# Column sums of squares held for all four of their squares, and the sixth pair of up blocks in seven products

## The chip, the cores and the metric

The kernel runs on one core of one Trainium2 chip. The metric is the device time of one execution in microseconds (us). A difference of about 0.3% is the least that a measurement of this kernel can tell from none. The engines are named as the profile names them: PE (TensorE; PEld are its weight loads), ACT (ScalarE), DVE (VectorE), POOL (GpSimd) and SP (SyncE, here a DMA queue). Matmuls have a fixed operand (128x128, loaded first) and a moving one.

## The reference, cut to what matters

One inference step of a two-layer decoder on 512 prompt tokens and 8 x 4 sample tokens (TOK = 544 columns, D_MODEL = 1024, D_FF = 2816). Every layer is a token mixer (causal pooling in layer 0, an HGRN2 recurrence in layer 1) and a gated feed-forward part with a short convolution, with RMS norms around both. All is float32.

```python
def rmsnorm(x, g):
    r = lax.rsqrt(jnp.mean(xf * xf, axis=-1, keepdims=True) + EPS)
    return (xf * r * g.astype(jnp.float32)).astype(x.dtype)

def conv_ffn(h, ctx, w_up, conv_w, conv_b, w_down):
    u = h @ w_up                                   # 1024 -> 2 * 2816
    full = jnp.concatenate([ctx.astype(u.dtype), u], axis=1)
    c = conv_b + sum(full[:, j:j + L] * conv_w[j] for j in range(CONV_W))
    gate, val = jnp.split(c, 2, axis=-1)
    y = (jax.nn.gelu(gate, approximate=True) * val) @ w_down

def trunk(...):
    for li in range(DEPTH):
        h = rmsnorm(x, norm_mix_pre[li])
        m = pool_mixer(...) or hgrn_mixer(...)
        x = x + rmsnorm(m, norm_mix_post[li])
        h = rmsnorm(x, norm_ffn_pre[li])
        m, st = conv_ffn(h, ffn_ctx[li], ...)
        x = x + rmsnorm(m, norm_ffn_post[li])
```

## The kernel before, in words

**Layout and precision.** Activations lie transposed: channels on 128 partitions, the 544 tokens along the free axis, eight such tiles for D_MODEL. A float32 matmul is done as three in the faster fp32r form: a value is split into a high part (ACT rounds it) and a low part (DVE subtracts the high part), and high x high, high x low and low x high are summed in PSUM (`mm3`, lines 516 to 520). Weights are split in the same way, in units of up to 128x512 (`ensure_units`, lines 444 to 477): SP loads a raw tile, ACT writes `wh`, DVE writes `wl`. There are ten buffers of each, and the code keeps nine units ahead of PE. Some blocks are split by transfers instead (`by_dma`, lines 430 to 432, with the windows `DW` of line 56): POOL issues a DMA that writes `wh`, ACT writes the negative of `wh` into `wl`, and POOL issues a second DMA that adds the weight to it (lines 460 to 463). DVE has no part in that.

**The feed-forward part** (`ffn`, from line 917). Its 22 pairs of up blocks (gate and value) come in parts of 6, 4, 4, 3 and 5 (`PARTS`), each followed in time by the down blocks of the part before. Pairs 0 to 2 are done by `group` in two column halves, pairs 3 to 5 of the first part by `block` (lines 522 to 530): 8 k-tiles x 2 halves x 3 products for each block, so 96 matmuls of 256 or 288 columns for a pair. All later pairs (`j >= SEVEN`, which is 6) are done by `seven` (lines 1058 to 1094): a 2 x 2 scheme of Winograd's kind with seven products of 4 k-tiles x 3, so 84 matmuls of 272 columns for a pair. That needs sums and differences of the operands, made once by `operands` (lines 1029 to 1046: `a`, `w`, and the `z` and `s` parts, which are kept whole in `hold`), and split by `both` (lines 1048 to 1050: ACT the high part, DVE the low part). It needs sums of the weights too, made by `seventh` (lines 479 to 498) with accumulating transfers into a raw tile `B_` and one DVE addition each for units 2 and 5; unit 6 uses a raw tile `C_`. Units 0, 4 and 6 of the seven are plain quarters of the weights. The operands are made while pairs 4 and 5 run (lines 1136 to 1139). The high and low parts of `z` and `s` (lines 1140 to 1144) go into tiles that the ordinary pairs still read, so they start when the last ordinary matmul is done; in the first product that uses `z` (the fifth) PE needs them.

**The residual steps** (`Residual`, lines 732 to 798) join two parts of a layer: for each half of the columns the mixer's or feed-forward's output is normalized, added to x (DVE), scaled and split (ACT `xh` or `oh`, DVE `xl` or `k`), and squared (ACT). `colsums` (lines 650 to 655) adds the squares over channels on PE: for each of the eight tiles one matmul with 32 columns of ones, tile k into the 32 partitions at `k % 4 * 32`, so that four neighbouring tiles use four different column quarters of PE and the second four are added to the first. Their total goes through ACT (`t<-pr`), a reciprocal root on DVE and PE again, and becomes `R`, by which the up blocks' results are multiplied. In the profile these matmuls are `pr<-t,cs 128*32`; the trace shows two records for each.

**The order of work** is planned. `Plan.record` (lines 127 to 159) notes every instruction with what it must follow; `Plan.emit` (lines 192 to 312) plays them through with a cost for each and picks, for the engine that is free first, the ready instruction with the longest tail of work behind it; PE takes matmuls that touch `pr` first (`urgent`, line 255). The order within each engine's queue is fixed by that; on the chip each instruction then waits for its own data alone. `plan.after(x)` (lines 118 to 123) adds, for the planner, that the next instruction follows the last writer of x. In `colsums` each of the four matmuls is held for its own square and for the last square of its four (line 654).

Of the kernel before, what the change touches and what calls it, by code (L numbers as in the profile page):

```python
# [11 lines left out]
F32 = _mybir.dt.float32  # L12
F32R = _mybir.dt.float32r
I32 = _mybir.dt.int32
AF = _mybir.ActivationFunctionType
ALU = _mybir.AluOpType

P = 128
# [18 lines left out]
PARTS = (6, 4, 4, 3, 5)  # L37

MIX = ((4, 4, 0, 0), (3, 3, 2, 0), (3, 3, 2), (2, 2, 2, 2, 0))

SEVEN = PARTS[0]

EARLY = 5

# [9 lines left out]

COLD = 7.0
DW = ((2, 12), (3, 32), (3, 12))
PACE = 0.25
HK = (0, 0, 0, 3, 5, 7, 27, 39)
GRP_U = 6
# [286 lines left out]
def trunk_step(ctx: ExitStack, tc: _tile.TileContext, xT, xp, xs, spool, s0, fctx, par, gb0, cst, bands,  # L346
               pw, wup, wdn, win, wout, yT, yB, o_pp, o_ps, o_hp, o_hs, o_ff):
    nc = tc.nc
    plan = Plan(tc)
    PE, DVE, ACT, POOL, SP = (plan.engine(*e) for e in (  # L350
        ("PE", nc.tensor), ("DVE", nc.vector), ("ACT", nc.scalar), ("POOL", nc.gpsimd), ("SP", nc.sync)))
# [10 lines left out]
    def tt(shape=(P, TOK), dt=F32):  # L362
        return tp.tile(list(shape), dt, tag="t", name="t")
# [11 lines left out]
    stream = []  # L375
# [3 lines left out]
    def add_up(li, j):  # L379
        up_i[li, j] = len(stream)  # L380
        if j < SEVEN:
            stream.append((wup[li, j], KT))
# [45 lines left out]
    bases = (0, min(hin_i.values()), up_i[1, 0])  # L428

    def by_dma(i):  # L430

        return any(lo <= i - b < hi for (lo, hi), b in zip(DW, bases))
    prepared = {}
    special = {}
    units = [(i, q) for i, (_, kc) in enumerate(stream) for q in range(-(-kc // 4))]
# [2 lines left out]
    raws, casts = {}, {}  # L438
    sums = {}

    def ensure(upto):
        ensure_units(unit0.get(upto + 1, len(units)) - 1)

    def ensure_units(upto):
        while nxt[0] <= min(upto, len(units) - 1):
            i, q = units[nxt[0]]
            nxt[0] += 1
            src, kc = stream[i]
            chunks = prepared.setdefault(i, [])
            n = min(4, kc - 4 * q) * P  # L450
            if i in special:
                sp, at = special[i]
                wh, wl = sp[at + q], sp[at + 2 + q]
            else:
                wh = wp.tile([P, 4 * P], F32R, tag="wh", name="wh", bufs=10)
                wl = wp.tile([P, 4 * P], F32R, tag="wl", name="wl", bufs=10)
            chunks.append((wh, wl))
            if by_dma(i):

                h, l, w = wh[:, 0:n], wl[:, 0:n], src[:, q * 4 * P:q * 4 * P + n]  # L460
                POOL.dma_start(h, w)
                ACT.activation(l, h.bitcast(F32), AF.Identity, scale=-1.0)
                POOL.dma_start(l, w, accum_op=ALU.add)
                continue
            if kc == 28:
                r = seventh(i, q)
            else:
                if q == 0:
                    raws[i] = tt((P, 512)) if kc * P <= 512 else wp.tile([P, KT * P], F32, tag="raw", name="raw")
                    if kc * P <= 512 and nxt[0] - 1 - EARLY in casts:  # L470

                        plan.held = {casts[nxt[0] - 1 - EARLY]}
                    SP.dma_start(raws[i][:, 0:kc * P], src)
                r = raws[i][:, q * 4 * P:q * 4 * P + n]
            casts[nxt[0] - 1] = len(plan.ops)
            ACT.activation(wh[:, 0:n], r, AF.Identity)
            DVE.tensor_tensor(wl[:, 0:n], r, wh[:, 0:n].bitcast(F32), op=ALU.subtract)

    def seventh(i, q):

        H = 4 * P
        lo, hi = slice(0, H), slice(H, 2 * H)
        w0, w1 = stream[i][0]
        if q == 0:
            B_, A_ = [wp.tile([P, KT * P], F32, tag="raw", name="raw") for _ in range(2)]
            raws[i] = A_, B_, sums[i % 2] if sums else tt((P, H))
            SP.dma_start(B_[:, hi], w1[:, lo])
            POOL.dma_start(B_[:, hi], w1[:, hi], accum_op=ALU.add)  # L490
            SP.dma_start(A_, w0)
            SP.dma_start(B_[:, lo], w0[:, lo])
            POOL.dma_start(B_[:, lo], w1[:, lo], accum_op=ALU.add)
            SP.dma_start(raws[i][2], w1[:, hi])
        A_, B_, C_ = raws[i]
        if q in (2, 5):
            DVE.tensor_tensor(B_[:, hi], B_[:, hi], A_[:, lo if q == 2 else hi], op=ALU.add)
        return (A_[:, lo], B_[:, hi], B_[:, hi], B_[:, lo], A_[:, hi], B_[:, hi], C_)[q]
# [23 lines left out]
    def block(i, rH, rL, kc, cut=HT, tick=None):  # L522

        t = ps2()
        for k in range(kc):
            for hf, sl in enumerate((slice(0, cut), slice(cut, TOK))):
                mm3(t[:, hf, 0:sl.stop - sl.start], i, k, rH, rL, sl, k == 0, k == kc - 1)
                if tick:
                    tick()
        return t  # L530
# [80 lines left out]
    def x_of(k, sl=slice(0, TOK)):  # L611
        return xt[k // 2][:, k % 2, sl]
# [3 lines left out]
    def pcol(off):  # L616
        return prm[:, off:off + 1]
# [32 lines left out]
    def colsums(pn, sqs, ks):  # L650

        for k in ks:
            j = k % 4 * 32
            plan.after(sqs[ks[-1]])
            PE.matmul(pn[j:j + 32], ones[:, 0:32], sqs[k], start=(k < 4), stop=(k >= 4), skip_group_check=True)

    def spread(dg, out):
# [259 lines left out]
    def ffn(li, XH, XL, res, enter, mtag, leave, n_ahead, homes, hv=HV):  # L917
# [35 lines left out]
        def evac_full(u, us, ps):  # L953
            DVE.tensor_tensor(u[:, 2:2 + SEQ].rearrange("p (a c) -> p a c", a=2), ps[:, :, 0:HP],
                              R[:, 0:SEQ].rearrange("p (a c) -> p a c", a=2), op=ALU.mult)
            DVE.tensor_tensor(us[:, :, 2:6], ps[:, 1, HP:HP + NS].rearrange("p (b t) -> p b t", t=NL), Rs, op=ALU.mult)
# [72 lines left out]
        def operands(k, out):  # L1029

            za, hold = tt(), out["hold"]
            zb, w, s_ = hold[:, k], hold[:, 6 + k % 2], hold[:, 4 + k // 2, U[k % 2]]
            for z, f in ((za, k), (zb, k + 4)):
                DVE.scalar_tensor_tensor(z, x_of(f), pcol(gn + f), R, op0=ALU.mult, op1=ALU.mult)
                SP.dma_start(yT[:, f], x_of(f))
            DVE.tensor_tensor(w[:, U[0]], za[:, U[1]], zb[:, U[1]], op=ALU.subtract)
            DVE.tensor_tensor(w[:, U[1]], za[:, U[0]], za[:, U[1]], op=ALU.subtract)
            DVE.tensor_tensor(za[:, U[1]], za[:, U[0]], w[:, U[0]], op=ALU.subtract)
            DVE.tensor_tensor(s_, zb[:, U[0]], za[:, U[1]], op=ALU.subtract)
            both(out["a", k], za)  # L1040
            if k % 2:

                h, l = (big.tile([P, 2, TOK], F32R, tag=f"X{q}", name="op") for q in (k // 2, 2 + k // 2))
                for e in range(2):
                    out["w", k - 1 + e] = h[:, e], l[:, e]
                    both(out["w", k - 1 + e], hold[:, 6 + e])

        def both(hl, src):
            ACT.activation(hl[0], src, AF.Identity)
            DVE.tensor_tensor(hl[1], src, hl[0].bitcast(F32), op=ALU.subtract)  # L1050

        def operand(q, k):
# [46 lines left out]
        def ahead_units(u):  # L1099
            ensure_units(min(u + 9, end))  # L1100
# [14 lines left out]
        def up(j):  # L1115
            if j >= SEVEN:
                seven(j)
                return
            for b in (j, NPAIR + j):
                i = up_i[li, b]  # L1120
                ahead_units(unit0[i])
                t = block(i, rH, rL, KT, HP)
                u, us = new_u(b, None if li == 0 and j < 8 else t[:, 0, 0:HP])
                evac_full(u, us, t)
                finish(u, us, b)
# [4 lines left out]
            y = [ys[starts[pi] + k] for k in range(PARTS[pi])]  # L1130
            do_down(pi, o, block(i, lambda k, sl: y[k][0][:, sl], lambda k, sl: y[k][1][:, sl], PARTS[pi]), None)

        up(GRP_U // 2)
        out, late = homes()
        out["hold"] = big.tile([P, KT, TOK], F32, tag=mtag, name="hold")
        for j in range(GRP_U // 2 + 1, PARTS[0]):
            for k in range(2):
                operands(2 * (j - GRP_U // 2 - 1) + k, out)
            up(j)
        late(out)  # L1140
        for k in range(4):
# [3 lines left out]
        rest = rp.tile([P, TOK], F32, tag="R", name="sums")  # L1145
        sums.update({0: rest[:, 0:4 * P], 1: fst[:, 2 * NPAIR * 18:2 * NPAIR * 18 + 4 * P]})
        mtile = big.tile([P, KT, TOK], F32, tag=mtag, name="m")
        for pi in range(1, len(PARTS)):
            for kind, q in mixed(pi):
                if kind == "down":  # L1150
                    down(pi - 1, q)
                else:
                    up(q)
            if pi == 1 and li == 0:
                plan.after(mtile[:, KT - 1, :])
                lower_bounds()
                POOL.memset(A, 0.0)
                POOL.memset(qm, 0.0)
                POOL.memset(Asp, 0.0)
# [6 lines left out]
        n, j0 = PARTS[LP], starts[LP]  # L1166
# [13 lines left out]
        for o in range(2, KT - GRP_D):  # L1180
            i = dn_i[li, LP, o]
# [449 lines left out]
    for kind, h in hgrn_order[GRP_U:]:  # L1631
        i = hin_i[kind, h]
        ensure(i + LOOK)
        while kind == "g" and "on" not in hd[h]:
            pending.pop(0)()
        pace[1] = PACE
        t = block(i, rH, rL, KT, HP, tick)
# [154 lines left out]
```

## Time and profile before

| | us |
|---|---|
| median of 3 runs | 1161.19 (1158.90 to 1162.99) |
| the profiled execution, its own time | 1161.18 |
| its span, first to last instruction | 1159.3 |
| PE busy | 1143.8 |
| DVE busy | 870.1 |
| ACT busy | 685.8 |
| POOL busy | 406.4 |

The profiled execution's time is the median of the runs to 0.01 us; 1.9 us of it lie outside the span. In the profile nearly every instruction has line 312, where the planner issues it, so groups are told by tile names: `out<-in`. `pa` and `ps` are the PSUM tiles of ordinary work, `pr` those of the norms; `op`, `hold`, `k`, `xl` hold operands; `wh` and `wl` the weight parts. A timeline row gives start, length, engine, what was done and, in brackets, idle time before it and what ended that. In the chain of waits each row gives start, length, engine and tile, and xN for N instructions merged.

### The profile page before, as it was taken

The numbers are of one execution on the slowest core, as the hardware profiler recorded it, in microseconds if no ns is written. First come the engines' busy times: TensorE is split into PE (matmuls) and PEld (weight loads), VectorE is DVE, ScalarE is ACT, GpSimd is POOL, SyncE is SP. The second block draws the span as 40 slices with busy tenths as digits, with TensorE's granted clock in tenths as the row PEclk, the third lists the DMA queues.
The fourth block names the chain that finished last, engine by engine and source line by source line (L and its number), as shares of the span: only waits on it lengthen the run. The fifth ranks groups of instructions, "written<-read, shape, count | busy, mean of one in ns | idle before, by whom it ended". The sixth has DMA issues, their size and how long they took to land.

```text
span 1159.3 us, 26118 instructions
## 1 busy us (share of the span) xinstructions
PE 1143.8 (99%) x9860; PEld 1104.2 (95%) x9860; DVE 870.1 (75%) x2068; ACT 685.8 (59%) x1459; POOL 406.4 (35%) x729
## 2 busy tenths in 40 slices
PE   8999999999999999999999999999999999999996
PEld 7789999999999998999999999979999999999996
DVE  6679977988788776576766785458986897878865
ACT  4546555656566575566666764455565665656653
POOL 3435222433443332443443420224621434343322
PEclk9999999999999999999999999999999999999999
DMA  9876167676876765777667642573536767777543
GB/s 317 206 189 133 55 175 178 169 179 171 195 172 159 206 208 115 156 149 162 154 157 154 135 127 101 149 188 79 132 83 187 190 167 180 174 169 192 115 127 77
DMA packets 90397, 183.48 MB, mean 158 GB/s; under 512 B 10522, under 2 KB 17050, under 8 KB 90264
## 3 DMA queue, kind: packets, MB, share of 16 engines
q0 software_dynamic: 48272, 91.90, 40.0%
q1 hardware_dynamic: 41856, 89.88, 23.7%
q8 instruction: 77, 1.26, 0.4%
q14 instruction: 48, 0.39, 0.1%
q10 hardware_dynamic: 144, 0.05, 0.0%
HBM read 156.00 MB, written 12.77 MB: 146 GB/s over the span
## 4 chain that ended last, share of the span: by engine, by line
PE 96%; DMA 1%; DVE 1%; ACT 1%; issue 0%; SPq 0%; POOL 0%; DVEq 0%; ACTq 0%; POOLq 0%
PE pa L312 47%; PE ps L312 46%; PE pr L312 3%; DMA t<-bands 1%; DMA wh<-win 0%; DVE t L312 0%; ACT A L312 0%; DVE x L312 0%; ACT t L312 0%; DVE m L312 0%; SPq L312 0%; DVE c L312 0%; ACT wl L312 0%; POOL t L312 0%; DVEq L1772 0%
## 5 line engine op out<-in xcount | busy, mean ns | idle before, releaser
L312 ACT ACTIVATE wh<-raw 128x512 fp32r<-128x512 f32 (+2 forms) x280 | 163.9, 598 | 158.5 <-PE pa L312 59.7
L312 PE MATMUL pa<-op,wh 128*128 128x272 f32 x1152 | 255.7, 288 | 0.0
L312 PE MATMUL ps<-t,wh 128*128 128x272 f32 x1248 | 236.5, 288 | 0.0
L312 DVE TENSOR_TENSOR wl<-raw,wh 128x512 fp32r<-128x512 f32 (+2 forms) x280 | 179.1, 652 | 75.3 <-ACT wh L312 73.2
L312 PE MATMUL pa<-op,wl 128*128 128x272 f32 x768 | 221.2, 288 | 0.0
L312 PEld LDWEIGHTS ps<-t,wh 128*128 128x128 f32 x1248 | 195.9, 188 | 0.0
L312 PEld LDWEIGHTS pa<-op,wh 128*128 128x128 f32 x1152 | 192.9, 188 | 0.0
L312 PE MATMUL ps<-t,wl 128*128 128x272 f32 x624 | 179.5, 288 | 0.0
L312 POOL COPY fst<-t 128x16 f32<-128x16 f32 (+1 forms) x176 | 92.8, 581 | 246.3 <-DVE t L312 246.2
L312 DVE TENSOR_TENSOR t<-t 128x512 f32<-128x512 f32 (+10 forms) x331 | 138.5, 441 | 45.6 <-ACT t L312 23.7
L312 PE MATMUL ps<-xh,wh 128*128 128x256 f32 (+1 forms) x560 | 165.7, 297 | 0.0
L312 PE MATMUL ps<-xl,wh 128*128 128x256 f32 (+1 forms) x560 | 162.3, 290 | 0.0
L312 PE MATMUL ps<-xh,wl 128*128 128x256 f32 (+1 forms) x560 | 161.1, 288 | 0.0
L312 DVE SCALAR_TENSOR_TENSOR t<-t,prm 128x560 f32<-128x560 f32 (+1 forms) x184 | 141.1, 796 | 4.6 <-ACT t L312 3.6
L312 PEld LDWEIGHTS pa<-op,wl 128*128 128x128 f32 x768 | 144.4, 188 | 0.0
L312 PE MATMUL pa<-k,wh 128*128 128x272 f32 (+2 forms) x560 | 137.4, 289 | 0.0
L312 PEld LDWEIGHTS ps<-t,wl 128*128 128x128 f32 x624 | 117.5, 188 | 0.0
L312 ACT ACTIVATE t<-t 128x544 fp32r<-128x544 f32 (+5 forms) x145 | 85.0, 596 | 44.0 <-DVE t L312 42.3
L312 PEld LDWEIGHTS ps<-xh,wh 128*128 128x128 f32 x560 | 105.2, 188 | 3.8 <-issue 0.9
L312 PEld LDWEIGHTS ps<-xl,wh 128*128 128x128 f32 x560 | 105.5, 188 | 2.6 <-issue 2.0
L312 PEld LDWEIGHTS ps<-xh,wl 128*128 128x128 f32 x560 | 105.4, 188 | 2.5 <-issue 2.4
L312 PEld LDWEIGHTS pa<-k,wh 128*128 128x128 f32 x560 | 97.5, 188 | 1.3 <-issue 1.3
(208 smaller groups left out, 2501.9 us busy)
## 6 DMA issues: line engine op xcount, KB each, us to landing
raw<-wup SPq DMA_DIRECT2D x37, 512.0 KB, 3.2
raw<-wup SPq DMA_DIRECT2D x64, 256.0 KB, 3.8
raw<-wup POOLq DMA_DIRECT2D x64, 256.0 KB, 5.8
wh<-win POOLq DMA_DIRECT2D x58, 256.0 KB, 3.4
wl<-win POOLq DMA_DIRECT2D x58, 256.0 KB, 4.7
m<-t POOLq DMA_DIRECT2D x48, 272.0 KB, 6.2
wh<-wup POOLq DMA_DIRECT2D x34, 256.0 KB, 4.2
wl<-wup POOLq DMA_DIRECT2D x34, 256.0 KB, 5.9
```

Of the source, the lines that this page charges most:

```text
L312: o[1](*o[3], **o[4])
```

## The change

Three things. In `colsums` each of the four matmuls is held, for the planner, for all four squares instead of its own and the last. `SEVEN` becomes 5: the sixth pair (pair 5) of each layer is done in seven products, so its two blocks leave the stream as ordinary blocks split by transfers and come back as one entry with seven units; the operands are made while pairs 3 and 4 run instead of 4 and 5. And part of the splitting goes to transfers: the low parts of the `a` operands k = 0 to 2 and of the `w` operands k = 0 and 1 (`EA`, `EW`), and units 0, 4 and 6 of the seven for the first three entries of seven in each layer (pairs 5, 6 and 7, `NSPLIT`); these three load no `C_`.

```diff
-SEVEN = PARTS[0]
+SEVEN = 5
...
+NSPLIT = 17
+EA = lambda k: k < 3
+EW = lambda k: k < 2
...
-        return any(lo <= i - b < hi for (lo, hi), b in zip(DW, bases))
+        return stream[i][1] < 28 and any(lo <= i - b < hi for (lo, hi), b in zip(DW, bases))
...
+    def split(h, l, w):
+        POOL.dma_start(h, w)
+        ACT.activation(l, h.bitcast(F32), AF.Identity, scale=-1.0)
+        POOL.dma_start(l, w, accum_op=ALU.add)
...
             if kc == 28:
-                r = seventh(i, q)
+                alone = i - (bases[2] if i >= bases[2] else 0) < NSPLIT
+                r = seventh(i, q, alone)
+                if alone and q in (0, 4, 6):
+
+                    src = src[q // 6][:, (0 if q == 0 else n):(n if q == 0 else 2 * n)]
+                    split(wh, wl, src)
+                    continue
...
-            raws[i] = A_, B_, sums[i % 2] if sums else tt((P, H))
+            raws[i] = A_, B_, None if alone else sums[i % 2] if sums else tt((P, H))
...
-            SP.dma_start(raws[i][2], w1[:, hi])
+            if not alone:
+                SP.dma_start(raws[i][2], w1[:, hi])
...
         for k in ks:
             j = k % 4 * 32
-            plan.after(sqs[ks[-1]])
+
+            plan.after(*(sqs[q] for q in ks))
...
-            both(out["a", k], za)
+            both(out["a", k], za, EA(k))
...
-                    both(out["w", k - 1 + e], hold[:, 6 + e])
+                    both(out["w", k - 1 + e], hold[:, 6 + e], EW(k))
 
-        def both(hl, src):
+        def both(hl, src, early=False):
             ACT.activation(hl[0], src, AF.Identity)
+            if early:
+
+                ACT.activation(hl[1], hl[0].bitcast(F32), AF.Identity, scale=-1.0)
+                POOL.dma_start(hl[1], src, accum_op=ALU.add)
+                return
             DVE.tensor_tensor(hl[1], src, hl[0].bitcast(F32), op=ALU.subtract)
...
-        up(GRP_U // 2)
         out, late = homes()
         out["hold"] = big.tile([P, KT, TOK], F32, tag=mtag, name="hold")
-        for j in range(GRP_U // 2 + 1, PARTS[0]):
+        for j in range(GRP_U // 2, SEVEN):
             for k in range(2):
-                operands(2 * (j - GRP_U // 2 - 1) + k, out)
+                operands(2 * (j - GRP_U // 2) + k, out)
             up(j)
...
+        for j in range(SEVEN, PARTS[0]):
+            up(j)
```

More of the change, by code (lines that the diff above doesn't have):

```diff
@@ L458, in ensure_units @@
             if by_dma(i):
[L460 to L463, printed above, removed]
+                split(wh[:, 0:n], wl[:, 0:n], src[:, q * 4 * P:q * 4 * P + n])
                 continue
             if kc == 28:
-                r = seventh(i, q)
+                alone = i - (bases[2] if i >= bases[2] else 0) < NSPLIT
[4 more added lines that the diff above has]
+                    continue
             else:
@@ L477, in ensure_units, with seventh @@
             DVE.tensor_tensor(wl[:, 0:n], r, wh[:, 0:n].bitcast(F32), op=ALU.subtract)
-    def seventh(i, q):
+    def seventh(i, q, alone):
         H = 4 * P
```

## The prediction

> **What bounds the kernel.** I read the page first, for who is busy and what the chain of waits consists of.
>
> ```profile
> span 1159.3 us, 26118 instructions
> ...
> PE 1143.8 (99%) x9860; PEld 1104.2 (95%) x9860; DVE 870.1 (75%) x2068; ACT 685.8 (59%) x1459; POOL 406.4 (35%) x729
> ...
> PE 96%; DMA 1%; DVE 1%; ACT 1%; issue 0%; SPq 0%; POOL 0%; DVEq 0%; ACTq 0%; POOLq 0%
> ```
>
> PE is busy for 99% of the span and is 96% of the chain. So a microsecond of PE work taken out is a microsecond won, as long as no other engine becomes late in its place. Both parts of the change take PE work out. The rest is to see how much, and what is next.
>
> **The sixth pair.** In the chain of waits in order of time, layer 1 shows pairs 3 to 5 as one row and the first pair of seven products as the next:
>
> ```profile
> 807.00 36.16 PE ps L312 x288
> 843.16 10.55 PE pa L312 x84
> ```
>
> An ordinary matmul costs 36.16 / 288 = 0.1256 us and so does one of the seven (10.55 / 84). A pair goes from 96 to 84 of them: 12.05 us becomes 10.55, so 1.5 us less in each layer, 3.0 us in all.
>
> **The column sums.** The same view, at the first residual step of the HGRN layer, second half of the columns:
>
> ```profile
> 442.43 4.64 PE ps L312 x40
> 447.07 0.60 PE pr L312 x2
> 447.68 0.43 PE ps L312 x2
> ...
> 453.88 0.60 PE pr L312 x2
> ```
>
> Here a column sum (two records) stands alone among ordinary matmuls. It takes 0.60 us itself, and the two matmuls behind it take 0.43 us where 40 undisturbed ones take 4.64 / 40 = 0.116 each: 0.20 us more. A visit to the column sums costs 0.80 us. From 447.07 to 453.88 there are seven such visits for eight sums (one row has two sums in 0.61 us). What a visit with four sums costs shows in the step of layer 0:
>
> ```profile
> 43.23 0.56 PE pr L312 x4
> ...
> 46.95 0.62 PE pr L312 x8
> 47.58 0.55 PE ps L312 x3
> ...
> 70.20 0.61 PE pr L312 x4
> ```
>
> At 46.95 four sums (eight records) take 0.62 us, as much as one, and three matmuls behind them 0.55 us instead of 0.35, again 0.20 more: 0.82 us. They run beside each other, since each uses its own quarter of the columns. That one is of the pooling step, where fours stand together already. The residual step's own sums from 43.23 to 70.20 come in 12 visits, six in each half; in the first half a visit with 256 columns takes 0.55 or 0.56 us, with the 0.20 then 0.75.
>
> Why they stand apart follows from the planner: the last square of a four is held by all four sums, so it has the longest tail and ACT does it first; each of the other sums becomes ready with its own square, a third of a microsecond apart, and two or three ordinary matmuls fit between. Held for all four squares, the four become ready together, and PE prefers them (`urgent`). So I expect two visits where there are six or seven. Layer 1's step has the same picture:
>
> ```profile
> 753.28 0.55 PE pr L312 x2
> ...
> 780.68 0.60 PE pr L312 x2
> ```
>
> From 753.28 to 780.68 there are six visits in the first half and seven in the second. The sum: layer 0's step 6 x 0.75 - 2 x 0.76 = 3.0 and 6 x 0.80 - 2 x 0.82 = 3.2; the HGRN step's second half 7 x 0.80 - 1.64 = 4.0; layer 1's 3.0 and 4.0. Together 17 us.
>
> The HGRN step's first half gives nothing:
>
> ```profile
> 432.00 2.62 ACT L312 ACTIVATE t<-x 128x256 f32<-128x256 f32 x8 [0.83 <-DVE x L312]
> ...
> 432.47 2.82 PE L312 MATMUL pr<-t,cs 128*32 128x256 f32 x16 [0.86 <-ACT t L312]
> ```
>
> There PE has nothing else to do, its eight sums stand together and follow ACT's eight squares one by one; ACT sets the end. I cost it at 0; the bounds are half a microsecond to either side, if ACT gets another order.
>
> Does something else hold these halves back when PE gets ahead? The next row is ACT's in the step whose second half was shown above:
>
> ```profile
> 454.52 0.41 ACT L312 ACTIVATE t<-pr 128x288 f32<-128x288 f32 x1 [4.47 <-PE pr L312]
> ```
>
> ACT stood idle for 4.47 us for the last column sum, with the scaled copies of x for the remaining channel tiles queued behind. So the chain that feeds PE's next half is itself behind the scattered sums, and moves up with them. The cover is real: the sums' new wait for four squares queues only PE's ordinary matmuls behind it, and they were behind it before. A stall at a four, if ACT is late by one square, is at most a third of a microsecond.
>
> **The hand-over to the seven products** is where the change can lose. Between `R` and the first seven, DVE is nearly full in both layers (the windows view; columns are busy us and instructions by engine, then clock and DMA):
>
> ```profile
> 78.20:129.20 51.00, 51.00 (x406) 51.00 (x405) 48.48 (x96) 30.98 (x49) 23.99 (x40) 1.00 0.56 119
> ...
> 788.30:843.20 54.90, 54.90 (x432) 54.90 (x431) 51.36 (x103) 32.63 (x51) 30.89 (x54) 1.00 0.51 111
> ```
>
> DVE has 2.5 us to spare of 51.0, and 3.5 of 54.9. The change shortens both windows by an ordinary pair, 12.05 us. What leaves DVE, by the groups view:
>
> ```profile
> L312 DVE TENSOR_TENSOR wl<-raw,wh 128x512 fp32r<-128x512 f32 (+2 forms) x280 | 179.1, 652 | 75.3 <-ACT wh L312 73.2
> ...
> L312 DVE SCALAR_TENSOR_TENSOR t<-t,prm 128x560 f32<-128x560 f32 (+1 forms) x184 | 141.1, 796 | 4.6 <-ACT t L312 3.6 <-issue 0.4
> ...
> L312 DVE TENSOR_TENSOR t<-ps,R 128x512 f32<-128x512 f32 (+1 forms) x88 | 35.2, 431 | 14.4 <-PE ps L312 13.8
> ...
> L312 DVE TENSOR_TENSOR op<-hold,op 128x544 fp32r<-128x544 f32 x8 | 5.7, 717 | 0.0
> ```
>
> The ordinary pair's own evacuation (4 x 0.431) and convolution (4 x 0.796) move behind the hand-over: 4.9 us. Five operand low parts go to transfers: 3.6 us. Three weight low parts of the first seven go too: 2.0 us. That is 10.5 us against 12.05, so of the 2.5 and 3.5 us some 0.9 and 1.9 remain. Not counted are the pair's products and their low parts, and the weights that only the later units need; they add a few microseconds of room. So DVE just holds, as it just holds now. The last step is short as well:
>
> ```profile
> 843.90 3.91 DVE L312 TENSOR_TENSOR k<-hold,op 128x544 fp32r<-128x544 f32 x6
> ```
>
> The low parts of `z` and `s` start when the ordinary matmuls end (843.16) and are done at 847.81; PE needs `z` after four products of 12 x 0.1256 = 1.5 us, at 849.2. That slack of 1.4 us stays, since the two sevens have the same shape.
>
> The transfers that are added (two for each of three units in three sevens, five for operands, in each layer, all on POOL's queue) are priced by these rows (KB, then median us to landing):
>
> ```profile
> m<-t POOLq DMA_DIRECT2D x48, 272.0 KB, 6.2
> wh<-wup POOLq DMA_DIRECT2D x34, 256.0 KB, 4.2
> wl<-wup POOLq DMA_DIRECT2D x34, 256.0 KB, 5.9
> ```
>
> An operand's accumulation takes about 6.2 us, of the same size; the last by transfer is made a pair ahead, so it is hidden, unless POOL is late by more than about 6 us. A split unit takes 4.2 + 0.65 for the cast (nearest row: DVE's low part) + 5.9 = 10.8 us from the moment its buffers are free. Ten buffers mean that this is nine units before its use: in ordinary pairs 27 us, but in two sevens in a row 9 x 1.507 = 13.6 us. Only pair 6 follows a seven directly, so its units 4 and 6 have 2.8 us to spare, in both layers. [...] POOL can be held besides:
>
> ```profile
> 112.09 1.44 POOL L312 COPY fst<-t 128x2 f32<-128x2 f32 x2 [4.84 <-DVE t L312]
> ```
>
> A copy that waits 4.84 us for DVE holds all transfers queued behind it; if such a copy falls in front, a unit is late by 4.84 - 2.8 = 2.0 us. With two units in two layers this stage costs between 0 and 8 us. I take 2, nearer to zero, since the planner places those copies where it expects their data. What lies after the hand-over on DVE is lighter: units 0, 4 and 6 of pairs 6 and 7 save it 2.0 us each, against less than 1 us more for a seven's evacuation.
>
> **The sum**, against the profiled execution: 1161.2 - 3.0 - 17.0 + 2 = 1143 us.
>
> **The rivals.**
>
> *The split units come late* (chance 0.17). Pair 6's units 4 and 6, and with more delay the operands too, wait behind POOL: 4 to 10 us instead of 2, so 1145 to 1151. For it speak the 2.8 us and POOL's waits of up to 4.84; against it that these are the only tight units, and that PE shows no wait for a weight by transfer in the pairs before. [...]
>
> *The sums don't come together, or their gain is taken by a wait* (0.08): the planner breaks the fours up, or DVE's normalization sets the pace of the halves. Then 3.0 us remain, about 1158. The 4.47 us of ACT's idle time speak against it.
>
> *DVE becomes the bound at the hand-over* (0.06). If the operands are finished no sooner than now, because the planner lets finished pairs go first, PE idles where the sixth pair ran, up to 12.05 us in each layer: 1143 - 2 + 24 = 1165, slower. It decides once DVE's work ahead of `z` exceeds the shortened windows of 39 and 43 us; the sum above says 38.0 and 40.9.
>
> **How the numbers follow.** My forecast, both savings with stalls of 0 to 4 us, has 0.69 and gives 1141 to 1145, with a measurement's spread of 2 us 1139 to 1147. The range reaches down to 1138 for the half microseconds left at 0, and up to 1153 to take in the late units. Faster by over 0.3% (below 1157.7): 0.69 + 0.17 and a little of the second rival, 0.87. Within 0.3%, which is what a measurement of this kernel can tell: 0.07. Slower: 0.06.
>
> **What would show it.** Right: 24 matmuls fewer in the ordinary groups; column sums in rows of x8, two for each half, in all but the HGRN step's first half; ACT's waits for `pr` shorter by 3 to 4 us each; `R` of layer 0 about 6 us earlier; a row of 84 right behind pair 4, and 84 behind that. Wrong: PE idle for `wl` or `op` within 21 us of the end of pair 4 (first or third rival: by POOL's queue or DVE's), column sums still in rows of x2, or PE idle for `xl` or `k` in the second halves.

## The result, and the profile after

The changed kernel takes 1141.60 us (median of 5 runs, 1140.96 to 1143.62) against 1160.78 (5 runs): a ratio of 0.9842, 95% interval 0.9826 to 0.9857, so 18.3 us less (the two medians lie 19.2 us apart). The forecast was 1143.0. The profiled execution took 1143.62 us, its span 1141.8 where it was 1159.3. From the page:

```profile
span 1141.8 us, 26147 instructions
...
PE 1123.7 (98%) x9836; PEld 1095.9 (96%) x9836; DVE 864.1 (76%) x2064; ACT 693.8 (61%) x1479; POOL 425.7 (37%) x763
...
PE 86%; issue 5%; DMA 4%; POOL 3%; ACT 1%; DVE 1%; SPq 0%; DVEq 0%; POOLq 0%; ACTq 0%
```

PE has 24 matmuls fewer and 20 us less to do, and it is still the bound (98%). That the chain names more DMA and POOL matters little: PE was busy beside most of that time.

**The column sums.** The timeline of PE at the HGRN step's second half, in which seven visits stood before:

```profile
439.87 0.40 PE L316 MATMUL ps<-xh,k 128*128 128x256 f32 x2
440.20 0.69 PE L316 MATMUL pr<-t,cs 128*32 128x288 f32 x8
440.82 0.38 PE L316 MATMUL ps<-xl,k 128*128 128x256 f32 x1
441.05 0.28 PE L316 MATMUL ps<-xh,k 128*128 128x256 f32 x1
...
442.32 0.69 PE L316 MATMUL pr<-t,cs 128*32 128x288 f32 x8
442.94 0.39 PE L316 MATMUL pa<-xl,wh 128*128 128x256 f32 x1
```

Two visits with eight records (four sums) each. A visit costs what was forecast: from 440.20 to 440.82 there are 0.62 us, and 0.1 us more than usual lies on either side. Rows of x8, two for a half, stand in every half that the prediction named; the first halves of layer 0's and of layer 1's step:

```profile
42.90 0.64 PE L316 MATMUL pr<-t,cs 128*32 128x256 f32 x8
...
47.41 0.64 PE L316 MATMUL pr<-t,cs 128*32 128x256 f32 x8
...
744.35 0.64 PE L316 MATMUL pr<-t,cs 128*32 128x256 f32 x8
746.43 0.64 PE L316 MATMUL pr<-t,cs 128*32 128x256 f32 x8
```

In PE's order over the whole program, 37 visits became 15. ACT's rows behind the last sum of the second halves, in order of time (layer 0's `R` after the first):

```profile
64.15 0.41 ACT L316 ACTIVATE t<-pr 128x288 f32<-128x288 f32 x1 [0.42 <-PE pr L316]
70.55 0.41 ACT L316 ACTIVATE R<-pr 128x288 f32<-128x288 f32 x1 [3.35 <-PE pr L316]
...
443.16 0.41 ACT L316 ACTIVATE t<-pr 128x288 f32<-128x288 f32 x1 [0.55 <-PE pr L316]
...
765.20 0.41 ACT L316 ACTIVATE t<-pr 128x288 f32<-128x288 f32 x1 [0.55 <-PE pr L316]
```

The idle time at 443.16 is 0.55 us where it was 4.47.

**The sixth pair and the hand-over.** The chain of waits in order of time:

```profile
110.38 16.80 PE pa L316 x134
...
157.84 7.13 DMA wl<-wup
165.01 1.52 PE pa L316 x10
...
790.38 24.11 PE ps L316 x192
814.49 16.83 PE pa L316 x134
```

Pairs 3 and 4 are 24.11 us, and the seven of pair 5 starts right behind them without a gap, in both layers; 134 is its 84 matmuls and 50 of pair 6, between whose others the first down blocks stand. The windows from `R` to the end of pair 4 show how full DVE (third column) is:

```profile
70.96:110.38 39.42, 39.42 (x314) 39.42 (x313) 37.93 (x77) 27.15 (x43) 26.30 (x40) 1.00 0.84 175
771.84:814.49 42.65, 42.65 (x335) 42.65 (x334) 39.56 (x80) 29.63 (x47) 29.47 (x50) 1.00 0.82 170
```

37.93 of 39.42 us, and 39.56 of 42.65. The only new wait of PE in the feed-forward parts comes later; the timeline of PE's weight loads:

```profile
165.01 0.19 PEld L316 LDWEIGHTS pa<-op,wl 128*128 128x128 f32 x1 [1.17 <-DMA wl<-wup]
```

That is unit 6 of pair 7 in layer 0, the last of the pair's three split units: 74 of its 84 matmuls stand ahead of the wait. POOL's and ACT's rows show where the time went (units 4 and 6 are the x2):

```profile
144.82 1.42 POOL L316 DMA_DIRECT2D wh<-wup  x2
...
157.84 0.88 POOL L316 DMA_DIRECT2D wl<-wup  x1 [0.78 <-ACT wl L316]
```

```profile
156.08 0.94 ACT L316 ACTIVATE wh<-raw 128x512 fp32r<-128x512 f32 x2 [1.36 <-DMA raw<-wdn]
156.92 0.62 ACT L316 ACTIVATE wl<-wh 128x512 fp32r<-128x512 f32 x1
```

The unit's `wh` was issued at 145.36 and landed at 150.25, but ACT wrote its negative only at 156.92, behind casts of down weights for whose raw tiles it had waited. Then the accumulating transfer took 7.13 us to land. From the first issue to the last landing that is 19.6 us.

### The profile page after: what moved, and what is told of

It is laid out like the page before. It is cut to its first block, busy times and chain, and to the rows that moved or that the text cites. A ratio compares the mean times of both kernels' runs of the same rounds, so it can differ in the third digit from the quotient of the medians.

```text
span 1141.8 us, 26147 instructions
## 1 busy us (share of the span) xinstructions
PE 1123.7 (98%) x9836; PEld 1095.9 (96%) x9836; DVE 864.1 (76%) x2064; ACT 693.8 (61%) x1479; POOL 425.7 (37%) x763
## 4 chain that ended last, share of the span: by engine, by line
PE 86%; issue 5%; DMA 4%; POOL 3%; ACT 1%; DVE 1%; SPq 0%; DVEq 0%; POOLq 0%; ACTq 0%
PE pa L316 45%; PE ps L316 39%; PE pr L316 1%; POOL wl L316 1%; DMA wh<-win 1%; DMA raw<-wup 1%; POOL wh L316 1%; DMA wl<-wup 1%; DMA k<-xp 1%; ACT A L316 0%; POOL t L316 0%; DVE t L316 0%; DMA o_hp<-t 0%; DMA raw<-wdn 0%; ACT t L316 0%
## 5 line engine op out<-in xcount | busy, mean ns | idle before, releaser
L316 PE MATMUL pa<-op,wh 128*128 128x272 f32 x1224 | 271.5, 288 | 0.0
L316 PE MATMUL pa<-op,wl 128*128 128x272 f32 x816 | 235.2, 288 | 1.0 <-DMA wl<-wup 1.0
L316 PEld LDWEIGHTS pa<-op,wh 128*128 128x128 f32 x1224 | 204.9, 188 | 0.0
L316 POOL COPY fst<-t 128x2 f32<-128x2 f32 (+1 forms) x176 | 92.0, 569 | 182.3 <-DVE t L316 182.2
L316 PE MATMUL ps<-xh,wh 128*128 128x256 f32 (+1 forms) x528 | 156.2, 297 | 0.0
L316 PEld LDWEIGHTS pa<-op,wl 128*128 128x128 f32 x816 | 153.4, 188 | 1.2 <-DMA wl<-wup 1.2
L316 PE MATMUL ps<-xl,wh 128*128 128x256 f32 (+1 forms) x528 | 152.7, 290 | 0.0
L316 PE MATMUL ps<-xh,wl 128*128 128x256 f32 (+1 forms) x528 | 151.4, 288 | 0.0
L316 PE MATMUL pa<-k,wh 128*128 128x272 f32 (+2 forms) x588 | 143.8, 289 | 0.0
L316 PEld LDWEIGHTS ps<-xh,wl 128*128 128x128 f32 x528 | 99.3, 188 | 2.1 <-issue 2.0
```

The source lines that it names most:

```text
L316: o[1](*o[3], **o[4])
```

## The experiments

The times of a run are compared with the kernel before on the same chip. Where stages are told, I measured them in the trace, from the start of one matmul to that of another.

**Each half of the change alone.** First the kernel before with the new hold:

```diff
-            plan.after(sqs[ks[-1]])
+            plan.after(*(sqs[q] for q in ks))
```

> The kernel before with the new hold in the column sums alone. Theory (PE is the bound, and a visit to the column sums costs 0.75 to 0.80 us whether it holds one sum or four): the order of PE now has 15 visits instead of 37, so 22 x 0.775 = 17 us less: about 1143.8 us against 1160.8. Rival (the sums give less, and the rest of the 19 us came from the sixth pair and what it moved): 1147 to 1152.

1142.82 us against 1161.81, ratio 0.9841 (0.9822 to 0.9860): the whole gain of the change. Then the changed kernel with the old hold (the reverse edit):

> The changed kernel with the old hold in the column sums: the sixth pair in seven products and the transfers alone. Theory: 3.0 us less for 24 matmuls, about 1 us of it lost to one late transfer, 38 visits to the sums: 1158 to 1159 us. Rival (the hand-over eats the gain): 1161 or more. Second rival (the sums gave less than counted): below 1155.

1160.78 us, ratio 0.9991 (0.9980 to 1.0003): nothing that can be told from none, though PE has the 24 matmuls fewer. The pages of the two runs, the sums alone first, then the sevens alone:

```profile
PE 1126.3 (99%) x9860; PEld 1099.1 (96%) x9860; DVE 869.8 (76%) x2068; ACT 684.6 (60%) x1459; POOL 409.2 (36%) x729
```

```profile
PE 1141.4 (98%) x9836; PEld 1100.1 (95%) x9836; DVE 864.3 (74%) x2064; ACT 693.0 (60%) x1479; POOL 424.6 (37%) x763
```

The new hold takes 17.5 us off PE's busy time (1143.8 before) and 17.7 off the span. The sevens take 2.4 off PE's busy time, with one visit more to the sums than before, but the span is 1.2 us longer (1160.5 against 1159.3): PE idles 3.6 us more. Part of that is the wait for the split weight, here from the groups of waits of PE's weight loads, a little longer than with the new hold:

```profile
PEld pa L316 <- DMA wl<-wup: 1.8, 1, 1.8
```

So all that the change gains in time comes from the column sums. The sixth pair's 3 us have to be looked for.

**More and fewer visits.** The kernel before without any hold between the squares (the `plan.after` line taken out), 56 visits expected instead of 37; the trace shows 54:

> The kernel before without any hold in the column sums: PE's order then has 56 visits, 19 more than before. Theory of the cost by visit: 19 x 0.775 = 14.7 us more, about 1175. Rival (what counts is when the last sum is done, not how many visits there are): the last sum of a half is no later than before, so within 2 us of 1160.8.

1174.35 us, ratio 1.0107 (1.0090 to 1.0124). The HGRN step's second half now has eight visits, each with ordinary matmuls between; three of them in PE's timeline:

```profile
458.10 0.67 PE L312 MATMUL pr<-t,cs 128*32 128x288 f32 x2
459.13 0.67 PE L312 MATMUL pr<-t,cs 128*32 128x288 f32 x2
460.17 0.67 PE L312 MATMUL pr<-t,cs 128*32 128x288 f32 x2
```

The span is 13.3 us longer for the 17 visits more, 0.78 us each (0.70 if there are 19); with the new hold it is 17.7 us shorter for 22 fewer, 0.80 each. The time goes with the visits, in both directions and at about the price that the rows gave (0.75 to 0.82).

Then the changed kernel with all eight sums of a half held for all eight squares and done in one visit (8 visits instead of 15):

```diff
-            plan.after(*(sqs[q] for q in ks))
+            plan.after(*(sqs[q] for q in range(KT)))
...
```

(In the lines left out `colsums` is called once a half, after the eighth square, with `range(KT)`.)

> The changed kernel with the eight sums of a half together, held for all eight squares: 8 visits instead of 15. If the cost of a visit is a fixed price of coming and going, 7 x 0.775 = 5.4 us less, about 1136. If it is a fixed 0.3 us and the rest is the streaming of its columns, which a second four has to repeat, 7 x 0.33 = 2.3 us less, about 1139.3. Rival (the first four then comes late, and with it the norm and the waiting ACT): no gain or a loss, 1141.6 or more.

1144.01 us, ratio 0.9856 (0.9836 to 0.9875): no gain over the fours. A visit with eight sums is not as cheap as one with four:

```profile
442.99 1.18 PE L316 MATMUL pr<-t,cs 128*32 128x288 f32 x16
444.10 0.39 PE L316 MATMUL pa<-xh,wl 128*128 128x256 f32 x1
```

From 442.99 to 444.10 there are 1.11 us, where two visits with four take 2 x 0.62. The second four costs 0.49 us: what is shared is 0.13 us, and the 0.2 us at the neighbours. That makes 7 x 0.33 = 2.3 us for the 7 visits, the second of the two sums in the expectation, and that isn't seen either. Where it goes isn't traced. The place where PE has nothing beside its sums, the HGRN step's first half, accounts for 0.1 us; this kernel and then the changed one:

```profile
426.98 1.64 PE L316 MATMUL pr<-t,cs 128*32 128x256 f32 x16 [2.04 <-ACT t L316]
```

```profile
424.65 2.79 PE L316 MATMUL pr<-t,cs 128*32 128x256 f32 x16 [0.84 <-ACT t L316]
```

Eight in a row take 1.64 us instead of 2.79, but they start only when ACT's eighth square is done (2.04 us of idle time), while single sums follow ACT one by one: counted from the last seven of layer 0, they end 0.1 us later.

**What the transfers are worth.** The changed kernel without split weights (`NSPLIT = 0`), then without operand transfers (`EA` and `EW` always false):

> The changed kernel with no weight unit of the sevens split by transfers: units 0, 4 and 6 of pairs 5 to 7 cast by ACT and subtracted by DVE, three times 0.65 us more on DVE ahead of the hand-over and as much in each of the next two pairs. Theory (DVE just holds, with 0.9 and 1.9 us to spare by the counted rows): PE waits 0 to 2 us in each layer, 1141 to 1145. Rival (DVE has room, the transfers only cost): 1140.4, by the 1.2 us of the one late transfer.

1146.32 us, ratio 0.9880 (0.9866 to 0.9894), 4.4 us slower than the changed kernel by the ratios. PE is not late at the hand-over (111 us); it waits for DVE afterwards, at 136, 188 and 200 us, and for 1.8 us in layer 1 (waits of PE's weight loads from 100 to 420 us):

```profile
PEld pa L316 <- DVE t L316: 2.3, 2, 1.3
PEld ps L316 <- DVE t L316: 0.8, 1, 0.8
```

> The changed kernel with all low parts of the operands made by DVE again: five times 0.72 us, 3.6 us more on DVE ahead of the hand-over in each layer. Theory: 1 to 3 us of waiting of PE for operands in each layer, 1143 to 1147. Rival (there was room): 1141.6.

1148.31 us, ratio 0.9886 (0.9869 to 0.9904), with single runs from 1144.46 to 1150.87, of which the profiled one is the slowest. Here, too, no operand is late. The profiled run loses at pair 7; two windows around its wait (the last three columns are granted clock, DMA share and GB/s):

```profile
165.00:170.90 5.90, 3.24 (x26) 3.01 (x25) 2.63 (x4) 3.85 (x7) 1.72 (x2) 1.00 1.01 259
170.95:174.36 3.41, 3.41 (x17) 3.41 (x16) 1.24 (x3) 1.09 (x2) 0.84 (x2) 0.50 0.68 167
```

PE's weight loads wait there for 2.9 us, again for the last split unit of pair 7, and then PE runs 3.41 us at half the clock: 1.7 us more, an estimate by half of the 3.41. These 4.6 us (1.2 in the changed kernel) are what the trace gives of the loss; the rest of it isn't traced. Both kinds of transfer help, but so far as the profiles show not by room at the hand-over: PE waits later, behind it.

**The late split weight.** Pair 7 goes back to ACT and DVE (`NSPLIT = 12`); pairs 5 and 6 stay as they are:

> The changed kernel with the split by transfers for pairs 5 and 6 only; pair 7, where the one wait for a low part by transfer was seen (1.2 us in layer 0), goes back to ACT and DVE. Theory: that wait goes and DVE has room there: 1140.4. Rival (the transfers of the downs around it are as late): 1141.6.

1140.75 us, ratio 0.9828 (0.9813 to 0.9844): the lowest of all, though its interval overlaps that of the changed kernel. From 100 to 420 us PE's weight loads wait for nothing at all. From the first column sum to the last seven of layer 0 it takes 368.8 us (371.4 in the changed kernel, 371.9 with the sums alone); but this profile has no stretch at half clock at its start, which is worth up to 1.7 us there by the same estimate (see the last section), so about 370.5 is to be compared: 1.4 less than with the sums alone, as the sixth pair should give.

**One step further.** The fifth pair in seven products as well (`SEVEN = 4`), all four operand steps while pair 3 runs:

```diff
-SEVEN = 5
+SEVEN = 4
...
-            for k in range(2):
-                operands(2 * (j - GRP_U // 2) + k, out)
+            for k in range(4):
+                operands(k, out)
```

> The changed kernel one step further: the fifth pair in seven products too, all four operands made while pair 3 runs. 24 matmuls fewer, 3.0 us. Theory (DVE is full ahead of the hand-over): its window shrinks by another 12.05 us in each layer while only 4.9 us of its work move behind it, so with 1 to 2 us to spare PE waits 5 to 6 us in each layer: 1148 to 1151. Rival (DVE has room that I didn't count, the pairs' products and their low parts): 1138.6 to 1142.

1158.29 us, ratio 0.9984 (0.9973 to 0.9996): the gain of the column sums is gone but for 2 us, with 24 matmuls fewer still. Waits of PE's weight loads from 100 to 420 us:

```profile
PEld pa L316 <- DVE t L316: 3.9, 3, 2.2
PEld ps L316 <- ACT m L316: 2.5, 1, 2.5
PEld pa L316 <- DMA wl<-wup: 2.2, 2, 1.8
...
PEld pa L316 <- ACT t L316: 0.7, 1, 0.7
PEld pa L316 <- DVE wl L316: 0.5, 1, 0.5
```

PE's weight loads wait for DVE, for ACT and for POOL's transfers, 11 us in layer 0 alone. With one pair more the engines that prepare the sevens set the pace in these places: much like the third rival of the prediction, one step later than it placed it, though DVE, which that rival named, has 4.4 of the 11 us.

**Where the sixth pair's 3 us go.** The seven of the sixth pair in one layer only, the other layer as before (`SEVENS = (5, 6)` for layer 0, `(6, 5)` for layer 1, with the transfers of that layer alone), and the sums alone once more on the same chip:

```diff
-        if j < SEVEN:
+        if j < SEVENS[li]:
...
+        if SEVENS[li] == 6:
+            up(GRP_U // 2)
         out, late = homes()
```

> The changed kernel with the sixth pair in seven products in layer 0 alone (12 matmuls more than the changed kernel, 12 fewer than the kernel before); layer 1 stands as in the kernel before, with the new hold of the column sums. Question: where the sixth pair's 3.0 us go. In the kernels measured so far the HGRN stage (first to last matmul of q and t) took 192.7 to 193.0 us in the three without the new sevens and 193.4 to 195.0 us in the six with them, though the order of the instructions is the same, and the end of the program (last matmul to the end) grew from 9.1-9.4 to 10.1-11.1 us with the number of POOL's DMA issues (358-360 against 382-402). Theory 1, what layer 0's sevens leave behind: layer 0 falls by 1.5 less a wait of 1 to 2 us for a transferred weight, the HGRN stage is again over 193.4 us, POOL's closing drain lies half way (10.3 to 10.9 us), so about the time of the kernel with the sums alone, ratio 0.984 to 0.986. Theory 2, the whole gain is there and only noise hides it: ratio 0.9825 to 0.983, the HGRN stage at 193.0.

> The changed kernel with the sixth pair in seven products in layer 1 alone; layer 0 stands as in the kernel before, with the new hold of the column sums. Theory 1, the HGRN stage suffers from what layer 0's sevens do ahead of it: here nothing has changed ahead of that stage, so it takes 192.7 to 193.0 us again; layer 1 gives its 1.4 us (331 against 332.4), the end grows by 0.3 to 0.5: ratio 0.983 to 0.984, about 1 us below the kernel with the sums alone. Theory 2, the stage's longer time comes with any change of the program (where the instructions and buffers lie): it is over 193.4 us here too.

> The kernel before with the new hold of the column sums alone, once more, on the same chip as the two kernels that have the sixth pair in one layer. HGRN stage 192.7 to 193.0 us, end after the last matmul 9.1 to 9.4 us, ratio 0.983 to 0.985. Theory 1: between the other two of this call or with the slower of them. Theory 2: 1.5 us above each of them.

Medians 1143.38, 1142.91 and 1142.59 us; ratios 0.9849 (0.9826 to 0.9872), 0.9840 (0.9821 to 0.9859), 0.9833 (0.9815 to 0.9852): none can be told from another. The stages of the traces can (us):

| stage | sums alone, again | layer 0 | layer 1 | changed kernel |
|---|---|---|---|---|
| first column sum to last seven of layer 0 | 371.9 | 372.1 | 371.8 | 371.4 |
| HGRN stage | 193.1 | 195.5 | 192.8 | 195.0 |
| last column sum to last seven of layer 1 | 332.3 | 332.5 | 330.8 | 331.0 |
| last matmul to the end | 9.6 | 9.4 | 10.4 | 10.1 |

Layer 1 gives its 1.5 us; layer 0 gives it and loses it again to the wait for pair 7's weight (1.8 us with layer 0 alone, 1.2 in the changed kernel). Two losses lie in stages that the change doesn't touch. The HGRN stage is 192.7 to 193.1 us in all five kernels whose layer 0 is as before, and 193.4 to 195.5 in all eight others, though the order of the instructions in it is the same on PE, DVE and ACT. In the two longest (the changed kernel and layer 0 alone) it grows most at one place; ACT's timeline of the changed kernel, and the same instruction with layer 1 alone:

```profile
563.72 0.63 ACT L316 ACTIVATE wl<-wh 128x512 fp32r<-128x512 f32 x1 [1.64 <-DMA wh<-win]
```

```profile
562.79 0.62 ACT L316 ACTIVATE wl<-wh 128x512 fp32r<-128x512 f32 x1
```

A weight by transfer lands later; ACT, and behind it DVE, are late by 1.7 us, and PE's weight loads wait 1.6 us for DVE at 568.40. So it is something that layer 0's sevens leave behind, as the first theory has it: the two groups of profiles, one for each kernel, don't overlap, though the nearest are only 0.4 us apart, and the sevens of layer 1 alone don't do it. Why that transfer lands late isn't shown: the median landing times in the stage are the same (3.1 to 3.4 us for `wh<-win`). It stays open.

The end grows with layer 1's transfers. POOL's closing drain (the last long record of its queue) takes 9.4 to 10.0 us in the four kernels without any new transfers and 9.5 without split weights, 10.5 with layer 0 alone (which doesn't lengthen the end), 10.7 to 11.8 with split weights in layer 1, and 12.3 with `SEVEN = 4`. In the kernel before it ended before SP's last wait; in the changed kernel it ends 0.9 us after it and is what the end waits for.

## Why the prediction was right, step by step

**The column sums: right, mechanism and size.** 17 us forecast; the sums alone have a span 17.7 us shorter. By step: layer 0's was to give 6.2 and gives 6.6 (378.44 to 371.87 us from its first sum to the last seven); the HGRN step's second half 4.0, measured 4.0 (85.06 to 81.04 from the last seven of layer 0 to the HGRN stage); layer 1's 7.0, measured 6.6 (102.5 to 95.9 from that stage to the last sum). The HGRN step's first half gives nothing, as costed: its eight sums still follow ACT. The second rival is out: the fours come together, and no wait took the gain. ACT's waits for `pr` fell by 2.9 us in layer 0, 3.9 in the HGRN step and 3.7 in layer 1, and layer 0's `R` comes 7.2 us earlier instead of about 6; 0.75 of that lies ahead of the first sum, where the change does nothing.

**The sixth pair: matmuls right, stalls in the wrong place and too low.** The step that failed is the +2 for stalls, with pair 6's units 4 and 6 as their cause. Those came in time. What was late is unit 6 of pair 7 in layer 0 (1.2 us), which the prediction had called safe since only pair 6 follows a seven directly. Its sum of 10.8 us for a split unit had no term for ACT's queue: between the landing of `wh` and ACT's negative of it there were 6.7 us, and the accumulating transfer took 7.13 us, not 5.9, so 19.6 us in all. The HGRN stage (+2.0) and the end (+0.8 against the kernel before) weren't in the sum at all. Together that is 4.0 us for the 3.0 that the pair saves, so about nothing remains, where the prediction counted 1. With the sums 0.7 us better the two misses partly cancel, and that the total is so near to 1143 is luck in part: in the profiles the first sum also comes 1.0 us earlier than with the sums alone (21.16 against 22.16), which is no work of the change.

**The hand-over: no wait, as forecast, but the sum for DVE isn't what shows it.** DVE was forecast at 38.0 us of 39 and 40.9 of 43, and is at 37.9 of 39.4 and 39.6 of 42.7; PE waits there for nothing, so the third rival didn't come. But DVE is as full in layer 0's window of the kernels without split weights and without operand transfers, which leave DVE 2.0 and 3.6 us of the work that the sum had taken off it:

```profile
71.12:111.20 40.08, 40.08 (x318) 40.08 (x317) 38.24 (x78) 27.97 (x45) 23.33 (x34) 1.00 0.66 139
```

```profile
73.44:112.86 39.42, 39.42 (x314) 39.42 (x313) 37.99 (x76) 22.85 (x37) 27.13 (x36) 1.00 0.65 137
```

PE doesn't wait at the hand-over there either. So other work of DVE gives way, the room was more than the 0.9 us of the sum, and that 38.0 was met says little for it. The low parts of the operands by transfer were priced at 6.2 us and landed in a median of 7.3 to 7.4 us in that window; they were early enough all the same.

The first rival had the split units late behind POOL's queue; pair 6's came in time. Beside a full DVE the transfers didn't land later: in layer 0's window of the changed kernel (70.96 to 110.38 us) `wl<-wup` lands in a median of 5.4 us with DVE 96% busy, against 5.9 us with DVE 95% busy in the window before the change (78.20 to 129.20 us).

**What would show it.** Behind pair 4 two rows of 84 were expected; the planner put down blocks into the second. The sign for late transfers was set too near: PE idle for `wl` within 21 us of the end of pair 4. The one wait for `wl` came 55 us behind it.

## What to carry to other kernels

Here four column sums that share PE by column quarters cost 0.82 us in one visit, and one alone 0.80: hold such matmuls until one is ready for each quarter. Holding them longer, for a second set, gained nothing here (ratio 0.9856, against 0.9842 with the fours). A planner that weighs each instruction by itself won't find this. And when a saving of a few microseconds is paid with transfers, look for the price in stages that the change doesn't touch (here 2.0 us in the HGRN stage and 0.8 at the end), and have a version of each half alone before the gain is put down to either.

## What the runs showed of the hardware

**A stretch at half the clock.** Rows of the windows view at the program's start: the kernel before, then the changed kernel without pair 7's split:

```profile
11.65:15.06 3.41, 3.41 (x17) 3.41 (x17) 0.77 (x3) 0.00 (x0) 0.72 (x3) 0.50 1.04 341
...
32.13:35.54 3.41, 3.41 (x17) 3.41 (x17) 1.63 (x5) 1.86 (x5) 0.24 (x3) 0.50 1.12 333
```

```profile
11.24:14.65 3.41, 3.41 (x29) 3.33 (x28) 0.95 (x3) 1.52 (x4) 0.72 (x3) 1.00 1.06 362
```

In 3.41 us PE starts 17 matmuls at a clock of 0.50 and 29 at 1.00. The kernel before and the changed kernel have two such stretches each in the first 40 us (the changed kernel's start at 11.24 and 31.72 us); without pair 7's split the clock is 1.00 for the first 60 us. A stretch can cost 1.7 us, an estimate by half of its length; two make 3.4 us, where the runs of the changed kernel differ by 2.7 us and those of the kernel before by 4.2.

Ahead of four stretches PE's matmuls had stood idle: for 3.31 us up to 11.02 in the kernel before, 2.76 us up to 10.28 in the changed kernel, 2.66 of the 5.90 us ahead of 170.90 without operand transfers, and 2.29 of the 9.00 us ahead of 149.00 with `SEVEN = 4`, where the clock is 0.50 from 150.00 to 153.30. The changed kernel's wait of 1.17 us at 165.01 was followed by none (the clock is 1.00 from 35.13 to 1134.20 us), nor was the 1.8 us with layer 0 alone (1.00 from 160 to 180). The stretch at 32 us of the kernel before had no idle time ahead of it: PE was busy for all of the 17 us from 15.10. So what sets a stretch off isn't shown. Where one follows a stall, the two are paid together: 2.9 us of waiting and 1.7 more without operand transfers.

**Quarters side by side.** Four sums in four column quarters start 7 ns apart (the changed kernel at 440.20 us) and cost 0.82 us with what they take from their neighbours; one sum costs 0.80. A second four behind them costs 0.49 us more (1.11 against 0.62 us, to the next matmul).
